# Attention's product with the values: from two half-array fp32 products to one full-array product of split operands

## Chip, core and metric

The kernel runs on one core of one Trainium2 chip, as one launch. The metric is the device time in microseconds (us) of that core, the median of several runs. Engines are named as in the profile: PE is TensorE (PEld its weight loads), DVE is VectorE, ACT is ScalarE, POOL is GpSimd, SP issues most of the DMAs.

## The reference, cut to what matters

The program is two small models in a row, both of width 1024 on 512 tokens, in float32: a block with windowed grouped-query attention, a block with retention (each followed by a gated feed-forward), and then two layers with a mixture of experts. Only the attention is touched. It has 16 query heads of 64 dimensions and 4 key/value heads; a block of 128 queries sees 256 context keys and up to three blocks of 128 local keys, and a sink column:

```python
s_ctx = einsum('bqkgd,bnkd->bkgqn', qb, k_c) * scale
s_loc = where(valid, einsum('bqkgd,bnkd->bkgqn', qb, kb) * scale, NEG_INF)
p = softmax(concatenate([s_ctx, s_loc, sink_col], axis=-1))
o = einsum('bkgqn,bnkd->bqkgd', p[..., :L], v_c) + einsum('bkgqn,bnkd->bqkgd', p[..., L:L + band], vb)
...
out_x = o_x @ w_o
```

The 256 context tokens are queries too (two more blocks, which see the context keys alone).

## The kernel before

**Split operands.** Most products are made from operands in two parts: `hi` is the value rounded to the type float32r, `lo` the remainder in the same type, and `mm3` adds up hi·hi, hi·lo and lo·hi in PSUM. `net.hilo(hi, lo, src)` makes the parts: ACT copies `src` into `hi`, then DVE subtracts `hi` from `src` into `lo`.

**Attention.** `Attention.heads` walks through 8 pairs of query heads (`pr`) and 6 query blocks (`b`) each, 48 blocks in all; `nk` is the number of local key blocks of a query block (2, 3, 3, 2, then 0 and 0 for the context). `nkt = 2 + nk` tiles of 128 keys follow, so a pair has 22 of them and the whole attention 176. The steps of a block:

- `scores`: PE writes the scores of both heads into the PSUM tile `sc`, of which there is one buffer (in pair 7 the last blocks use a smaller one). DVE takes the maximum (L1156) and three short operations on the tile `sm` (L1157 to L1159), ACT two exponentials (L1163) into `pt`; these are the last readers of `sc`.
- `weights`: two short DVE operations (L1171, L1172); then one head's weights are scaled on ACT (L1177), the other's on POOL (L1175).
- `values`: the weights are transposed on PE (L1192), up to two key tiles at a time into the PSUM tile `tr` (2 buffers), copied to `th` (ACT at L1197, or DVE at L1195 for the second piece), and multiplied with the values `vs` (L1205). There are 96 such pieces: 80 of 512 columns and 16 of 256. Then `hilo` splits the PSUM tile `po` into `oh` and `ol`.

The steps overlap: block n+1's scores are written before block n's `values`, and block n+1's `weights` are called from within it. `Fill` puts other PE work between them: the query projections of the next pair (L975 to L977, 3 x 8 matmuls), the projection of finished heads (`project`, L1127 on DVE), and adaptive-norm products (L491). The order in which each engine gets its instructions is set by the framework's scheduler when the program is built, so it can move when the costs of instructions change.

**The product at L1205** has one key tile's values of one group as weights, 128 keys by 64 columns in fp32. The two heads of a pair go to the array's two column halves (`tile_position=(0, 64 * s)`) and run beside each other. The program has 352 such matmuls; each fp32 one runs as two instructions of the trace, 704.

`begin` makes the values of the 6 token tiles in its generator `token_values`, and copies them out of PSUM at L1103.

Of the kernel before, what the change touches and what calls it, by code (L numbers as in the profile page):

```python
# [8 lines left out]
F32 = mybir.dt.float32  # L9
F32R = mybir.dt.float32r  # L10
BF = mybir.dt.bfloat16
I32 = mybir.dt.int32
AF = mybir.ActivationFunctionType
OP = mybir.AluOpType
# [4 lines left out]
S = 512  # L19
# [207 lines left out]
class Net:  # L227
    def __init__(self, ctx, tc, ins, out, taps=None):
        self.tc, self.nc, self.ins, self.out = tc, tc.nc, ins, out
        self.taps = taps or {}  # L230
        self.n = 0
        self.rings, self.st_rings = [], []
        self.ri, self.si = 0, {}
        self.clock, self.sides, self.inside = 0.0, [], False
# [698 lines left out]
class Attention:  # L933


    def __init__(self, net, hid, x, ctxT, gx, gc, fill, es, sp):
        self.net, self.hid, self.fill = net, hid, fill
        self.x, self.ctxT, self.gx, self.gc = x, ctxT, gx, gc
        self.wq = net.ins["attn_w_qkv"][0].rearrange("(k p) c -> p k c", p=128)
        self.wo = net.ins["attn_w_o"][0].rearrange("(k p) c -> p k c", p=128)  # L940
        self.op = es.enter_context(net.pool("attn_o"))
        self.es, self.ps_es, self.rope_es = ExitStack(), ExitStack(), ExitStack()
        self.ap = self.es.enter_context(net.pool("attn"))
        self.rp = self.rope_es.enter_context(net.pool("attn_rope"))
        self.sp = sp
        self.vs = [self.ap.tile([128, 4, 64], F32, name=f"vs{t}") for t in range(6)]
        self.small = False
        self.kh, self.kl, self.qs, self.qy, self.oh, self.ol = ({} for _ in range(6))

# [123 lines left out]
    def begin(self, first, ps_es):  # L1073

        net, nc = self.net, self.net.nc
        kw, qw = first
        wst = net.stage(self.wq[:, :, 1280:1536], 8, 256)
        pk, pq, pc = (self.sp.tile([128, S], F32, name=f"first{n}") for n in "kqc")
        ps = {1: (pk, pc[:, :L]), 0: (pq, pc[:, L:])}
        for g, (c0, n) in enumerate(GR):  # L1080
            for is_k, w in ((1, kw), (0, qw)):
                for us in self.product(ps[is_k][c0 // S][:, c0 % S:c0 % S + n], w, c0, n):
                    net.tick(us)
            if g == 0:
                self.consts()
                wv = net.split(wst[:, 0:4])
        rest = []
        for is_k, gain, then in ((1, "kg", self.keys_rest), (0, "qg", self.queries_rest)):
            if is_k:
                f, sq = (self.t(n, (128, NT), F32R, 3, self.op).bitcast(F32) for n in ("oh", "ol"))  # L1090
            else:
                f, sq = self.ftiles()
            self.take(ps[is_k][0], 0, S, f, sq, net.v(gain))
            self.take(ps[is_k][1], S, L, f, sq, net.v(gain))
            rest.append(then(0, f, sq))
        wv += net.split(wst[:, 4:8])
        rest = [net.side(r) for r in rest]

        def token_values():
            for t in range(6):  # L1100
                pv = net.ps()[:, :256]
                net.mm3(pv, [self.hid.at(k, t * 128, 128) + (wv[k // 4 * 2][:, k % 4], wv[k // 4 * 2 + 1][:, k % 4]) for k in range(8)])
                nc.scalar.activation(self.vs[t], pv.rearrange("p (g d) -> p g d", g=4), AF.Copy)  # L1103
                yield 2.6

        self.tv = self.fill.add(token_values(), -1)
        self.fill.pump(8.0)
        for r in rest:
            net.finish(r)
        ps_es.close()  # L1110
        self.sp = self.ps_es.enter_context(net.pool("attn_ps", space=PSUM))
# [67 lines left out]
    def values(self, pr, blkno, pt, beside, between=None):  # L1179
        net, nc, sp = self.net, self.net.nc, self.sp  # L1180
        q0, kb, nk, m0 = self.blocks[blkno]
        g, nkt = pr // 2, 2 + nk
        po = sp.tile([128, S], F32, name=net.nm("po"), tag="po")[:, :128]
        if blkno == 0:
            self.oh[pr] = self.t("oh", (128, NT), F32R, 3, self.op)
            self.ol[pr] = self.t("ol", (128, NT), F32R, 3, self.op)

        def turn(j0, n):
            tr = sp.tile([128, 2, 256], F32, name=net.nm("tr"), tag="tr", bufs=2)
            for j in range(j0, j0 + n):  # L1190
                for s, c in enumerate((j, j + 2 if j < nk else j - nk)):
                    nc.tensor.transpose(tr[:, j - j0, s * 128:s * 128 + 128], pt[s][:, c * 128:(c + 1) * 128], net.ident)  # L1192
            th = self.t("th", (128, 2, 256), bufs=3)
            if j0 == 2:
                nc.vector.tensor_copy(th[:, :n], tr[:, :n])  # L1195
            else:
                nc.scalar.activation(th[:, :n], tr[:, :n], AF.Copy)  # L1197
            return j0, n, th

        def take(j0, n, th):  # L1200

            for j in range(j0, j0 + n):
                v = self.vs[kb + j if j < nk else 4 + j - nk][:, g]
                for s in range(2):
                    nc.tensor.matmul(po[64 * s:64 * s + 64], v, th[:, j - j0, s * 128:s * 128 + 128],  # L1205
                                     start=(j == 0), stop=(j == nkt - 1), tile_position=(0, 64 * s))

        ready = []
        for j0 in range(0, nkt, 2):
            ready.append(turn(j0, min(2, nkt - j0)))  # L1210
            if j0 >= 2:
                take(*ready.pop(0))
        if between:
            between()
        self.fill.pump(beside)
        while ready:
            take(*ready.pop(0))
        net.hilo(self.oh[pr][:, q0:q0 + 128], self.ol[pr][:, q0:q0 + 128], po)

    def heads(self, beside, tail):  # L1220

# [50 lines left out]
def retention(net, hid, x_groups, before, freed, last, fill):  # L1272
# [3 lines left out]
    with ExitStack() as yes:  # L1276
# [201 lines left out]
        for hd in range(4):  # L1478
            tables(hd)
            qk(hd)  # L1480
            if hd:
                project(hd - 1)
                values(hd)
            pan = gate_panel(hd, 0)
            gated(hd, pan, attend())
# [563 lines left out]
def diff_attention(net, i, pool, sp, hh, hl, win, mix, V, lam_init, early, last):  # L2049
# [115 lines left out]
    for n, (hd, b) in enumerate(work):  # L2165
        if b == 0:
            fill.finish(nxt.get(hd))
            if hd == 0:
                fill.add(early, 1)
            if hd < 3:  # L2170
                nxt[hd + 1] = fill.add(project(hd + 1))
            if hd == 2:
                fill.finish(early)
        if (hd, b) == (3, 0):
            fill.add(last)
        ready.append((hd, b, scores(hd, b)))
        step_out()
        fill.pump(1.5 if hd < 3 else 1.8)
        if n:
            values(*ready.pop(0))  # L2180
    for r in ready:
        values(*r)
        step_out()
# [586 lines left out]
```

## Time and profile before

| | |
|---|---|
| median of 3 runs | 3113.56 us (3111.11 to 3114.87) |
| the profiled execution | 3106.33 us |
| its span, first to last instruction | 3104.2 us |
| mean granted clock of PE | 0.977 |
| PE busy over the span | 2939.8 us (95%) |
| blocks of the attention | about 88 to 445 us of the span |

The profile is of one execution, whose own time was 7 us below the median of the runs shown. A share of busy time is a mean over all stages, and the attention is about a ninth of the span.

### The profile page before, as it was taken

What the parts mean: (1) busy time and instruction counts of PE and PEld (TensorE: products, weight loads), DVE (VectorE), ACT (ScalarE), POOL (GpSimd) and SP (SyncE); (2) the same over time, 40 slices, a digit from 0 to 9 for tenths busy, and PEclk for the clock granted to TensorE, in tenths of its full rate; (3) what the DMA queues carried; (4) which work ended last, traced back from release to release, by engine and by line L of the source; (5) the groups of instructions that cost most, each with busy time, mean ns of one, the idle gap of its engine ahead of it and who ended that gap; (6) DMA issues with size and microseconds to landing.
All of it is one profiled execution on the core that took longest, in us unless ns stands there. A gap on an engine that the chain in (4) does not pass through costs nothing. (4 is left out here: it accounts for less than half of the span.)

```text
span 3104.2 us, 42345 instructions
## 1 busy us (share of the span) xinstructions
PE 2939.8 (95%) x16384; PEld 2427.0 (78%) x16384; DVE 1902.0 (61%) x3557; ACT 1298.5 (42%) x2227; POOL 406.0 (13%) x389
## 2 busy tenths in 40 slices
PE   6999989999999999999999999999999988999995
PEld 5777779888888888888887788877876767787663
DVE  5566575545552664535465543669778766988865
ACT  3655563121212432323243322436555543656544
POOL 1112130000000200000020000221212212121220
PEclk8999999999999999999999999999999989999997
DMA  6121133324441222223133432231469944146993
GB/s 223 49 74 55 49 98 100 116 89 129 144 142 55 88 67 82 78 67 98 37 114 117 125 127 96 89 119 41 133 201 362 351 161 121 35 153 226 378 352 142
DMA packets 307875, 410.18 MB, mean 132 GB/s; under 512 B 16655, under 2 KB 248207, under 8 KB 307025
## 3 DMA queue, kind: packets, MB, share of 16 engines
q1 hardware_dynamic: 293840, 357.03, 35.0%
q0 software_dynamic: 13824, 50.34, 4.5%
q8 instruction: 133, 2.18, 0.3%
q14 instruction: 78, 0.63, 0.1%
HBM read 379.01 MB, written 28.31 MB: 131 GB/s over the span
## 5 line engine op out<-in xcount | busy, mean ns | idle before, releaser
L308 ACT ACTIVATE hi<-st 128x1024 fp32r<-128x1024 f32 (+1 forms) x420 | 432.7, 1034 | 691.9 <-PE ps L369 497.6
L309 DVE TENSOR_TENSOR lo<-st,hi 128x1024 fp32r<-128x1024 f32 (+1 forms) x420 | 510.5, 1219 | 233.9 <-ACT hi L308 222.5
L368 PE MATMUL ps<-hxh,hi 128*128 128x512 f32 (+1 forms) x1280 | 477.3, 374 | 2.5 <-DVE sg L828 0.8
L369 PE MATMUL ps<-hxl,hi 128*128 128x512 f32 (+1 forms) x1280 | 475.3, 372 | 0.5 <-DVE hxl L645 0.5
L370 PE MATMUL ps<-hxh,lo 128*128 128x512 f32 (+1 forms) x1280 | 475.0, 371 | 0.0
L368 PEld LDWEIGHTS ps<-hxh,hi 128*128 128x128 f32 x1280 | 241.9, 189 | 52.2 <-ACT sg L827 5.6
L370 PEld LDWEIGHTS ps<-hxh,lo 128*128 128x128 f32 x1280 | 242.0, 189 | 42.4 <-issue 1.2
L369 PEld LDWEIGHTS ps<-hxl,hi 128*128 128x128 f32 x1280 | 242.1, 189 | 41.2 <-issue 1.2
L368 PE MATMUL ps<-ah,hi 128*128 128x256 f32 (+1 forms) x592 | 200.5, 339 | 3.2 <-DVE x L774 1.6
L369 PE MATMUL ps<-al,hi 128*128 128x256 f32 (+1 forms) x592 | 198.5, 335 | 0.2 <-DVE al L378 0.2
L370 PE MATMUL ps<-ah,lo 128*128 128x256 f32 (+1 forms) x592 | 198.4, 335 | 0.0
L774 DVE SCALAR_TENSOR_TENSOR x<-ps,vecs,x 128x512 f32<-128x512 f32 (+1 forms) x136 | 84.4, 623 | 147.9 <-PE ps L370 147.8
L828 DVE TENSOR_TENSOR sg<-sg,ps 128x512 f32<-128x512 f32 (+1 forms) x70 | 40.1, 572 | 187.0 <-PE ps L370 186.3
L593 POOL TENSOR_TENSOR nacc<-nacc,nsq 128x256 f32<-128x256 f32 x56 | 49.4, 883 | 594.7 <-ACT nsq L592 593.5
L368 PEld LDWEIGHTS ps<-ah,hi 128*128 128x128 f32 x592 | 111.4, 188 | 19.0 <-DVE x L774 3.6
L2571 PE MATMUL py<-st,at 128*128 128x512 f32 x272 | 123.0, 593 | 1.7 <-DVE y L2575 1.2
L369 PEld LDWEIGHTS ps<-al,hi 128*128 128x128 f32 x592 | 111.5, 188 | 12.6 <-DVE al L378 0.4
L370 PEld LDWEIGHTS ps<-ah,lo 128*128 128x128 f32 x592 | 111.3, 188 | 12.6
L2545 PE MATMUL pa<-hi,xt 128*128 128x512 f32 x288 | 118.5, 412 | 0.5 <-ACT xt L377 0.5
L368 PE MATMUL ps<-hch,hi 128*128 128x256 f32 x416 | 117.7, 283 | 0.6 <-DVE mod L527 0.5
L369 PE MATMUL ps<-hcl,hi 128*128 128x256 f32 x416 | 117.2, 282 | 0.0
L370 PE MATMUL ps<-hch,lo 128*128 128x256 f32 x416 | 117.1, 282 | 0.0
(671 smaller groups left out, 7065.7 us busy)
## 6 DMA issues: line engine op xcount, KB each, us to landing
st<-moe_w_dram SPq DMA_DIRECT2D x136, 512.0 KB
st<-ffn_w_in_dram SPq DMA_DIRECT2D x44, 1024.0 KB
st<-moe_w_dram SPq DMA_DIRECT2D x34, 1024.0 KB
ast<-ada_w_dram SPq DMA_DIRECT2D x56, 512.0 KB
st<-ret_w_qkvg_dram SPq DMA_DIRECT2D x24, 1024.0 KB
st<-ffn_w_out_dram SPq DMA_DIRECT2D x24, 768.0 KB
st<-ada_w_dram SPq DMA_DIRECT2D x12, 1024.0 KB
st<-w_in_dram SPq DMA_DIRECT2D x12, 1024.0 KB
```

The costliest lines, as they stand in the source:

```text
L308: self.nc.scalar.activation(h, v, AF.Copy)
L309: self.nc.vector.tensor_tensor(l, v, h.bitcast(F32), op=OP.subtract)
L368: self.nc.tensor.matmul(ps, wh, xh, start=(i == 0), stop=False)
L369: self.nc.tensor.matmul(ps, wh, xl, start=False, stop=False)
L370: self.nc.tensor.matmul(ps, wl, xh, start=False, stop=(i == n - 1))
L593: nc.gpsimd.tensor_tensor(self.acc, self.acc, sq, op=OP.add)
L774: net.nc.vector.scalar_tensor_tensor(xm, p, self.gate[:, m:m + 1], xm, op0=OP.mult, op1=OP.add)
L828: nc.vector.tensor_tensor(sg, sg, pu, op=OP.mult)
L2545: nc.tensor.matmul(pa, th[:, k], wh, start=(k == 0), stop=False)
L2571: nc.tensor.matmul(py[:, n * 512:n * 512 + 512], at[:, f], w2[f][:, 0, n * 512:n * 512 + 512], start=(f == 0), stop=(f == 1))
```

## The change

1. `vs` holds 128 columns for each token tile and group instead of 64: the values' `hi` part in columns 0 to 63 and the `lo` part in 64 to 127, made with `hilo`.
2. A transposed piece is split by `hilo` into `th` and `tl`: every piece now has one ACT copy and one DVE subtraction of its full width, where it had one copy on one of the two.
3. The product is two matmuls for each key tile, with the same weights (128 x 128), and moving 256 columns (both heads): one with `th`, one with `tl`. It writes a `po` of 128 x 256: the rows 0 to 63 hold the products with the values' hi part, 64 to 127 those with the lo part. All four terms are kept.
4. At the end of a block the two halves are added: for each head ACT copies one half of `po` into the new tile `ob` (one buffer), and DVE adds the other. `oh` is then copied from `ob` on ACT, and `ol` is subtracted on POOL.

```diff
-        self.vs = [self.ap.tile([128, 4, 64], F32, name=f"vs{t}") for t in range(6)]
+        self.vs = [self.ap.tile([128, 4, 128], F32R, name=f"vs{t}") for t in range(6)]
...
-                nc.scalar.activation(self.vs[t], pv.rearrange("p (g d) -> p g d", g=4), AF.Copy)
+                pv = pv.rearrange("p (g d) -> p g d", g=4)
+                net.hilo(self.vs[t][:, :, 0:64], self.vs[t][:, :, 64:128], pv)
...
-        po = sp.tile([128, S], F32, name=net.nm("po"), tag="po")[:, :128]
+        po = sp.tile([128, S], F32, name=net.nm("po"), tag="po")[:, :256]
...
-            th = self.t("th", (128, 2, 256), bufs=3)
-            if j0 == 2:
-                nc.vector.tensor_copy(th[:, :n], tr[:, :n])
-            else:
-                nc.scalar.activation(th[:, :n], tr[:, :n], AF.Copy)
-            return j0, n, th
-
-        def take(j0, n, th):
+            th, tl = (self.t(r, (128, 2, 256), F32R, bufs=2) for r in ("th", "tl"))
+            net.hilo(th[:, :n], tl[:, :n], tr[:, :n])
+            return j0, n, th, tl
+
+        def take(j0, n, th, tl):
...
-                for s in range(2):
-                    nc.tensor.matmul(po[64 * s:64 * s + 64], v, th[:, j - j0, s * 128:s * 128 + 128],
-                                     start=(j == 0), stop=(j == nkt - 1), tile_position=(0, 64 * s))
+                nc.tensor.matmul(po, v, th[:, j - j0], start=(j == 0), stop=False)
+                nc.tensor.matmul(po, v, tl[:, j - j0], start=False, stop=(j == nkt - 1))
...
-        net.hilo(self.oh[pr][:, q0:q0 + 128], self.ol[pr][:, q0:q0 + 128], po)
+        ob = self.t("ob", (128, 128))
+        for s in range(2):
+            a, b = self.HALVES[s]
+            cs = slice(s * 128, s * 128 + 128)
+            nc.scalar.activation(ob[a], po[b, cs], AF.Copy)
+            nc.vector.tensor_tensor(ob[a], ob[a], po[a, cs], op=OP.add)
+        oh, ol = (o[pr][:, q0:q0 + 128] for o in (self.oh, self.ol))
+        nc.scalar.activation(oh, ob, AF.Copy)
+        nc.gpsimd.tensor_tensor(ol, ob, oh.bitcast(F32), op=OP.subtract)
```

**What the change does to the order.** Behind the attention (PE's row 2214 of 14,562 before) the instructions of every engine stand in the same order as before; SP's queue differs only in where three of the loads of `ada_w` stand among the feed-forward's weights. Within the attention the scheduler moved rows. The lines of `values` have other numbers after the change: the transpose L1192 is L1193, the products are L1202 (with `th`) and L1203 (with `tl`), DVE's maximum L1156 is L1157, and so on by one; the copies and subtractions of a piece stand at the helper's lines L377 and L378, the two additions of a block at L1220.

PE in pair 0, block 1, from the last two transposes of the block's second piece on, before (`tr`, `th`, `po`, `vs` as above; `ps` is the next pair's query projection; x2 is a pair of half-array matmuls):

```order
L1192 MATMUL tr_884<-kident_69,pt_756 128x128
L1192 MATMUL tr_884<-kident_69,pt_757 128x128
L975 MATMUL ps_836<-hxh_110,hi_830 128x512
L1205 MATMUL po_876<-th_882,vs_344 64x128 x2
L1205 MATMUL po_876<-th_882,vs_345 64x128 x2
L1192 MATMUL tr_895<-kident_69,pt_756 128x128
L1192 MATMUL tr_895<-kident_69,pt_757 128x128
L976 MATMUL ps_836<-hxl_111,hi_830 128x512
L1205 MATMUL po_876<-th_889,vs_346 64x128 x2
L1205 MATMUL po_876<-th_889,vs_348 64x128 x2
```

and the same place of the change:

```order
L1193 MATMUL tr_901<-kident_69,pt_761 128x128
L1193 MATMUL tr_901<-kident_69,pt_762 128x128
L977 MATMUL ps_846<-hxh_110,lo_841 128x512
L1202 MATMUL po_891<-th_897,vs_344 128x256
L975 MATMUL ps_846<-hxh_110,hi_840 128x512
L976 MATMUL ps_846<-hxl_111,hi_840 128x512
L977 MATMUL ps_846<-hxh_110,lo_841 128x512
L975 MATMUL ps_846<-hxh_110,hi_840 128x512
L976 MATMUL ps_846<-hxl_111,hi_840 128x512
L1203 MATMUL po_891<-tl_898,vs_344 128x256
L1202 MATMUL po_891<-th_897,vs_345 128x256
L1203 MATMUL po_891<-tl_898,vs_345 128x256
```

The first product with `th` stands where it stood, the first with `tl` has five projection matmuls of 512 columns ahead of it.

DVE at the same place, from the maximum of block 2's scores to the reciprocal, before:

```order
L1156 TENSOR_REDUCE sm_851<-sc_852 128x2
L1195 COPY th_889<-tr_884 128x512
L1157 TENSOR_TENSOR sm_851<-sm_851,qys_590 128x2
L1158 TENSOR_TENSOR sm_851<-sm_851,nsink 128x2
L1159 TENSOR_TENSOR sm_851<-sm_851,nsink 128x2
L1171 TENSOR_TENSOR sm_851<-sm_851 128x2
L378 TENSOR_TENSOR ol_805<-po_876,oh_804 128x128
L1172 RECIPROCAL sm_851<-sm_851 128x2
```

and of the change:

```order
L1157 TENSOR_REDUCE sm_866<-sc_867 128x2
L378 TENSOR_TENSOR tl_898<-tr_892,th_897 128x512
L1158 TENSOR_TENSOR sm_866<-sm_866,qys_590 128x2
L378 TENSOR_TENSOR tl_907<-tr_901,th_906 128x512
L1159 TENSOR_TENSOR sm_866<-sm_866,nsink 128x2
L1160 TENSOR_TENSOR sm_866<-sm_866,nsink 128x2
L1172 TENSOR_TENSOR sm_866<-sm_866 128x2
L1173 RECIPROCAL sm_866<-sm_866 128x2
L378 TENSOR_TENSOR tl_918<-tr_914,th_917 128x256
```

Two subtractions of block 1's pieces now stand between the maximum of block 2's scores and the short operations that its exponentials wait for, where one copy stood; the subtraction that makes `ol` is gone from DVE here.

## Rows read from the trace of the kernel before

**Rows 1.** The page's head and its first part: busy time, share, instructions.

```profile
span 3104.2 us, 42345 instructions
PE 2939.8 (95%) x16384; PEld 2427.0 (78%) x16384; DVE 1902.0 (61%) x3557; ACT 1298.5 (42%) x2227; POOL 406.0 (13%) x389
```

**Rows 2.** Windows: the attention's blocks, then head pairs 0 and 4 (busy us).

```profile
88.00:445.00 357.00, 338.16 (x2494) 269.90 (x2493) 216.67 (x540) 208.73 (x497) 75.34 (x79) 0.98 0.20 63
...
90.50:131.10 40.60, 38.29 (x282) 30.12 (x282) 21.02 (x57) 24.31 (x60) 7.52 (x8) 0.96 0.22 66
...
270.40:316.50 46.10, 44.68 (x331) 37.77 (x329) 32.11 (x73) 25.03 (x58) 8.86 (x8) 1.00 0.17 52
```

The columns are the stretch, its length, the busy us of PE, PEld, DVE, ACT and POOL, the granted clock, the DMA share and GB/s.

**Rows 3.** Timeline of PE in pair 4: start, duration, line.

```profile
251.10 0.66 PE L1205 MATMUL po<-th,vs 128*64 128x128 f32 x8
251.69 0.38 PE L976 MATMUL ps<-hcl,hi 128*128 128x256 f32 x1
251.91 0.28 PE L977 MATMUL ps<-hch,lo 128*128 128x256 f32 x1
...
252.43 0.29 PE L1153 MATMUL sc<-kh,qs 128*128 128x256 f32 x1
252.64 0.44 PE L1205 MATMUL po<-th,vs 128*64 128x128 f32 x4
253.01 0.38 PE L1154 MATMUL sc<-kl,qs 128*128 128x256 f32 x1
253.23 0.28 PE L976 MATMUL ps<-hcl,hi 128*128 128x256 f32 x1
253.35 0.29 PE L977 MATMUL ps<-hch,lo 128*128 128x256 f32 x1
...
254.16 0.28 PE L975 MATMUL ps<-hch,hi 128*128 128x256 f32 x1
```

**Rows 4.** Instructions on tile po: count, min/median/max ns, first and last start.

```profile
L1205 PE MATMUL po<-th,vs x704: 272/273/476, 93.3 to 442.2; 128*64 128x128 f32 x176
```

**Rows 5.** Instructions on tile tr: prices of copies and subtractions from PSUM.

```profile
L378 DVE TENSOR_TENSOR xt<-tr,xt x72: 676/682/692, 2304.2 to 3045.1; 128x512 fp32r<-128x512 f32 x72
...
L2563 DVE COPY at<-tr x36: 412/420/427, 2316.5 to 3059.2; 128x256 f32<-128x256 f32 x36
L1195 DVE COPY th<-tr x32: 674/685/692, 93.5 to 430.5; 128x512 f32<-128x512 f32 x32
```

**Rows 6.** Groups by shape, 88 to 445 us: busy us, mean ns, idle before.

```profile
L378 DVE TENSOR_TENSOR ol<-po,oh 128x128 fp32r<-128x128 f32 x48 | 13.8, 288 | 14.4 <-ACT oh L377 14.2
...
L1197 ACT ACTIVATE th<-tr 128x512 f32<-128x512 f32 x48 | 28.5, 594 | 46.7 <-PE tr L1192 46.7
...
L377 ACT ACTIVATE oh<-po 128x128 fp32r<-128x128 f32 x48 | 12.9, 270 | 20.2 <-PE po L1205 19.8
...
L1000 POOL TENSOR_TENSOR qf<-qf,krc 128x512 f32<-128x512 f32 x8 | 13.8, 1719 | 28.8 <-DVE aux L999 16.2 <-DVE sm L1159 8.0 <-DVE sm L1157 4.6
...
L593 POOL TENSOR_TENSOR nacc<-nacc,nsq 128x256 f32<-128x256 f32 x14 | 10.4, 744 | 6.5 <-ACT nsq L592 5.7 <-DVE sm L1172 0.5
```

**Rows 7.** Waits of PE and PEld, 88 to 445 us: total us, times, longest.

```profile
PE sc L1149 <- ACT pt L1163: 7.4, 6, 1.9
...
PE po L1205 <- DVE th L1195: 2.8, 5, 0.7
PE po L1205 <- ACT th L1197: 1.9, 8, 0.3
...
PEld po L1205 <- ACT th L1197: 13.0, 29, 1.2
PEld sc L1149 <- ACT pt L1163: 10.1, 9, 2.0
...
PEld po L1205 <- DVE th L1195: 3.9, 5, 0.9
```

## The prediction

> **What bounds the kernel now.** I read the page first: PE is busy for 95% of a span of 3104.2 us, and DVE for 61% [rows 1]. Then the windows: in the attention's 357 us PE is busy for 338.2, DVE for 216.7, ACT for 208.7; a pair with little fill work (pair 0, 40.6 us) has DVE at 52% and ACT at 60%, one with a projection beside it (pair 4, 46.1 us) has DVE at 70% and PE still at 97% [rows 2]. So PE sets the pace, and a us of PE's work is a us of time as long as the other engines deliver. But "busy" counts a matmul's whole pipelined duration, so what a matmul costs is read from the timeline, as the distance of two starts. Last come the waits: PE and its loads wait for `th` for 21.6 us in 47 places (1.9 + 2.8 + 13.0 + 3.9), and for the exponentials that free `sc` for 17.5 us in 15 of the 48 blocks [rows 7]. The second number matters here: the score tile has one buffer, and the loop scores, maximum, exponentials, next scores is nearly as long as a block.
>
> **What the product costs on PE, before and after.** Full-array matmuls of 256 moving columns in a stream start 0.116 us apart (seven steps from 253.35 to 254.16) [rows 3]. A run of eight half-array instructions, two key tiles, takes 0.59 us to the next start (251.10 to 251.69), a run of four, one key tile, 0.37 us (252.64 to 253.01) [rows 3]. Each run also delays its neighbours: it starts 0.21 us after a 256-column matmul (252.43 to 252.64) where 0.116 is usual, and the matmul behind it is followed after 0.22 us (251.69 to 251.91, and 253.01 to 253.23) where 0.116 is usual [rows 3]. I read these as the array emptied, and a weight load exposed, when its division changes.
>
> After the change a key tile is two full-array matmuls of 256 columns like those of L976, so 0.232 us, and the runs have no borders. A long run loses 0.59 - 0.464 = 0.126, plus 0.094 and 0.104 at its borders: 0.324 us. A short one loses 0.37 - 0.232 = 0.138 and the same borders: 0.336. On the timeline of PE I counted 91 runs between 93.3 and 442.2 us, 65 of them of eight instructions and 14 of four [rows 4]. So **PE's work shrinks by 91 x 0.33 = 30 us**. The number of columns streamed does not shrink: within a run a key tile takes about 0.22 us (the difference of the two run lengths, 0.59 - 0.37), and 0.232 after. All of the gain is borders.
>
> One rule speaks against this. The Trainium skill, "TensorEngine Tiling (Array Packing)", sections "The Problem" to "When to Use Tiling", says that weights of 64 columns or fewer leave half the array unused and that column tiling gains up to 2x. By it, giving the halves up would double 176 x 0.22 = 39 us of products: some 39 us slower, 3153; I give that 0.02 of the slower cases' chance. The rows don't bear that out for this change, since the free half is filled with the values' low part and both heads share one stream; I take the 0.232. The weights change only at every second matmul, fewer than in L975 to L977, which hold 0.116, so no extra load is priced (its worst, the 0.22 of an exposed one at each of 352, would be +36 us).
>
> **What is added on the other engines.** DVE: 80 subtractions of 512 columns at 0.682 and 16 of 256 at about 0.42, less 32 copies at 0.685 [rows 5]: 54.6 + 6.7 - 21.9 = +39.4; 96 additions of 128 columns at the 0.288 of `ol`, less 48 of those [rows 6]: +13.8; six for `vs` at 0.42: +2.5. In all +55.7, to 272 us of 357, 76%. ACT: 32 more copies at 0.594 and 96 copies of 128 columns at 0.270 (`oh` remains) [rows 6]: +19.0 + 25.9 = +45, to 254 us, 71%. If the 64-partition operations cost half, DVE has 14 and ACT 13 us less; I take the full price, as the column count is the same as in those rows. POOL: 48 subtractions of 128 columns, between a quarter of 1.719 and half of 0.744 [rows 6], about 0.4 us, 19 us in all on an engine that is busy for 75 of 357 [rows 2]. Behind `ol` on POOL stands the scaling of a later block's weights; `ol` itself is read by a projection blocks later, so it hides.
>
> If every engine were free to run ahead, none of these would cost time: PE's rest, about 357 - 30 us, is longer than 272 or 254. Pair 4 shows that DVE at 70% lets PE run at 97% [rows 2]. What costs is order, in two places.
>
> *Waits for the pieces.* A product with `tl` waits for one more step, 0.682 us and a handover of some 0.05. Counting in the order, at the prices above, the PE work that stands between a piece's last transpose and its first use: median 1.4 us before, and 2.1 us to the first use of `tl`. So +0.73 needed, +0.66 covered by fill work; 0.07 x 96 = 7 us is the upper end, nothing the lower (uses of `th` now have more cover than before). I take +3.
>
> *The score loop.* In DVE's order, between the maximum and the third short operation, there stood 9 copies of `th` and 12 subtractions of `ol` over the 48 blocks, 9.6 us; after the change 24 subtractions of `tl` and 38 additions of `ob`, 24 x 0.682 + 38 x 0.288 = 27.3 us. So the loop grows by 17.7 us, 0.37 per block, while PE's part of a block shrinks by 30 / 48 = 0.62. In the 15 blocks in which PE already waited for the loop [rows 7], PE's gain is lost and the growth is paid: 15 x 0.62 + 15 x 0.37 = 15 us. The ends: nothing, if the loop's slack takes it; all 48 blocks, 48 x 0.99 = 47 us. I take +15.
>
> The six extra DVE operations for `vs` lie in the start, before the first scores; 1 us at most, left out. Behind the attention nothing moves.
>
> **Sum.** -30 + 3 + 15 = **-12 us**. The profiled execution (3106.3) would come to 3094; it was 7 us below the median of the runs, so the median goes from 3113.6 to **3101.5**.
>
> **Rivals.**
> - *PE's whole gain arrives* (-22 to -30 us, 3084 to 3092): the scheduler's fill covers `tl`, and the loop has slack. For it: pair 4 [rows 2]. Against: PE waited for `sc` in 15 blocks while DVE and ACT were at about 60%. Chance 0.17.
> - *Given back to the last few us* (within 0.2%, which is 6 us and about what a measurement here can tell from no change; 3107 to 3120): the score loop binds in 21 to 33 blocks instead of 15, at 0.62 + 0.37 each 21 to 33 us for the +15. For it: in the light pairs PE and ACT come close, in pair 0 ACT's 24.3 + 5.6 us against PE's 40.6 - 3.75. Chance 0.18.
> - *Slower*: evacuation becomes the bound. From block to block runs a second loop: transposes, `th`, `tl`, product, `ob`, and behind `ob` in ACT's queue the scaling of the next block's weights, which its transposes need. It grows by 0.73 for `tl`, and by about 0.5 since ACT now copies both pieces and copies `po` twice (0.270): 1.25 us per block. Where it binds, a block pays 1.25 instead of gaining 0.62; from 16 of the 48 blocks on the gain is gone, and with 24 the sum is +15, 3128. Against it: on ACT and DVE it holds 0.594 + 0.594 + 0.682 + 0.54 us and the scaling [rows 5, 6], while a block lasts 357 / 48 = 7.4 us. Chance 0.2. The Trainium skill states such an end: "TensorEngine Tiling (Array Packing)", "PSUM Bottleneck", says that the copy out of PSUM may become the bottleneck when the product gets faster, and that both ScalarE and VectorE should be used for it, as is done here; the trace before shows neither above 70%.
>
> **How the numbers follow.** The forecast, 3093 to 3107, has 0.45. Faster by over 0.2%: 0.45 + 0.17 = 0.62; same 0.18; slower 0.20. The range of 8 in 10 goes from 3087 (half of the first rival below it) to 3118 (half of the slower case above it), which leaves out about 0.18. The likeliest case's own range is 3093 to 3107.
>
> **What would show it right or wrong.** Right: L1202 and L1203 follow their neighbours after 0.12 us with no 0.2 us borders; the window of the attention is some 12 us shorter and the rest unchanged; waits for `tl` and `th` sum to about 25 us; waits for `sc` grow from 17.5 us to about 25 to 30. Wrong: products at 0.2 us or more apart; `sc` waits at 17 us or below (then the whole gain arrives); waits of the transposes on ACT or POOL that were not there (then the slower case); DVE's subtraction with one PSUM operand above 0.7 us.

## The result and the profile after

The change makes the kernel slower: 3129.14 us, the median of 6 runs (3127.21 to 3137.16), against 3110.96 us for 6 runs of the kernel before. The ratio is 1.0059, with a 95% interval of 1.0048 to 1.0070, so some 18 us. The prediction was 12 us faster.

The profiled execution took 3129.62 us, its span is 3127.4. First its page:

```profile
PE 2942.8 (94%) x16032; PEld 2442.9 (78%) x16032; DVE 1954.8 (63%) x3675; ACT 1342.4 (43%) x2355; POOL 428.2 (14%) x437
```

PE has 352 instructions less and is busy 3 us longer [rows 1]. The window of the attention, which now ends at about 462 us, has the columns of [rows 2]:

```profile
88.00:462.00 374.00, 342.13 (x2149) 288.69 (x2147) 266.88 (x657) 252.25 (x625) 97.11 (x127) 0.95 0.18 59
```

The window is 17 us longer; from the first transpose to the last product the attention is 14 us longer (table below). DVE has 50 us more and ACT 44, near what the prediction counted (55.7 and 45), and neither is near full: 71% and 67%. The granted clock fell from 0.98 to 0.95. Next the groups by shape that answer to [rows 5, 6]:

```profile
L378 DVE TENSOR_TENSOR tl<-tr,th 128x512 fp32r<-128x512 f32 x80 | 53.8, 686 | 8.3 <-ACT th L377 6.5
L1220 DVE TENSOR_TENSOR ob<-ob,po 64x128 f32<-64x128 f32 x96 | 27.2, 284 | 19.2 <-ACT ob L1219 17.0
...
L377 ACT ACTIVATE th<-tr 128x512 fp32r<-128x512 f32 x80 | 45.5, 594 | 25.7 <-PE tr L1193 25.6
...
L1219 ACT ACTIVATE ob<-po 64x128 f32<-64x128 f32 x96 | 26.0, 271 | 36.7 <-PE po L1203 23.5 <-DVE ob L1220 11.0 <-PE sc L1154 0.9
...
L1223 POOL TENSOR_TENSOR ol<-ob,oh 128x128 fp32r<-128x128 f32 x48 | 24.4, 508 | 89.6 <-ACT oh L1222 62.7 <-ACT sm L1165 21.9 <-PE ps L370 5.0
```

The prices on DVE and ACT came out as taken from the rows of before (0.682, 0.288, 0.594 and 0.270 us); POOL's `ol` takes 0.51 where the prediction put about 0.4. What an instruction costs was not the error; the error lies in when it can start. The waits, as in [rows 7] (total, times, longest); a wait that holds a matmul and its weight load appears in both rows, in part for the same time:

```profile
PE po L1203 <- DVE tl L378: 9.9, 14, 2.5
PE sc L1150 <- ACT pt L1164: 6.6, 8, 2.2
...
PEld po L1203 <- DVE tl L378: 16.4, 21, 2.7
PEld sc L1150 <- ACT pt L1164: 9.5, 11, 3.1
PEld po L1202 <- ACT th L377: 8.2, 22, 0.8
...
PEld tr L1193 <- ACT pt L1178: 2.9, 6, 0.7
PEld tr L1193 <- ACT ob L1219: 2.3, 2, 1.5
```

Counted once where the two rows hold the same time, the waits for `th` and `tl` are 24.6 us in 43 places, where those for `th` were 17.0 us in 34. Those of the first score matmul of a block (L1150, L1149 before) for the exponentials that free `sc` are 9.5 us in 11 blocks where they were 10.1 in 9: the score loop did not get worse. The longest single waits have grown from 1.2 us to 2.7 at the products. One of them on PE's timeline:

```profile
154.16 0.39 PE L1203 MATMUL po<-tl,vs 128*128 128x256 f32 x1 [2.13 <-DVE tl L378]
154.39 0.28 PE L1202 MATMUL po<-th,vs 128*128 128x256 f32 x1
154.51 0.28 PE L1203 MATMUL po<-tl,vs 128*128 128x256 f32 x1
```

The products themselves do what was forecast: 154.39 to 154.51 is 0.12 us, without borders. But PE stands still for 2.13 us, and the matmul behind the wait is followed only after 0.23 us (154.16 to 154.39). DVE around that time:

```profile
151.91 0.42 DVE L1061 TENSOR_SCALAR qys<-nry 128x12 f32<-128x12 f32 x1 [1.10 <-POOL nry L384]
...
152.44 0.95 DVE L1069 TENSOR_TENSOR qs<-qf,qs 64x768 fp32r<-64x768 f32 x1
153.42 1.29 DVE L378 TENSOR_TENSOR tl<-tr,th 128x512 fp32r<-128x512 f32 x2
```

`th` of the first piece was ready at 151.60, but the two `tl` stand in DVE's order behind the norms of the next pair's queries (`qys`, `qs`). DVE is idle for 1.10 us there, until POOL has the inverse roots (`nry`). Before the change the same wait of 1.10 us stood in the same place (150.80 on DVE), with one copy `th` and one short `sm` operation behind it instead of two subtractions, and PE waited for that copy for 0.41 us. The idle time is only a part of the 2.13 us: `qs` (0.95 us), which stood behind the copy before, now stands ahead of both `tl`. And behind the standstill, in windows again:

```profile
154.20:156.00 1.80, 1.80 (x16) 1.80 (x16) 0.51 (x1) 1.00 (x3) 0.00 (x0) 0.98 1.05 408
155.90:159.30 3.40, 3.40 (x12) 1.93 (x11) 2.28 (x12) 1.85 (x5) 0.69 (x1) 0.51 0.65 240
```

PE is busy without a gap from 154.20 on, yet from 155.90 to 159.30 it was granted 0.51 of its clock, the lower of its two levels (1.2 GHz). So the wait is paid again in part. The Trainium skill, "TensorE: Matmul & The Clock Gate", section "HAM oscillation — how this bites in real kernels", describes a loop in which each wait for a DMA is followed by matmuls at the throttled clock. The rows here agree that half clock follows a wait; the wait is one for DVE, though, and the fall comes 1.7 us after its end.

**PE's time in the attention** can be split along its timeline. The distance of two starts, less the price of the first in a stream (0.116 us for 256 columns, 0.229 for 512, and so on), goes to the wait or border between them, to the half clock where that was granted, or to a load that shows behind a wait. From the first transpose to the last product, in us of the profiled execution (one each, so a few us are chance; work includes the waits of the L491 products for their weights):

| kernel | work | borders | waits | behind a wait | half clock | rest | stage |
|---|---|---|---|---|---|---|---|
| before | 286.9 | 23.0 | 26.9 | 2.4 | 5.5 | 5.5 | 350 |
| after | 287.9 | 3.1 | 41.8 | 7.2 | 17.4 | 6.9 | 364 |
| pe_alone | 284.9 | 3.3 | 28.4 | 6.4 | 8.7 | 6.8 | 338 |
| load | 290.4 | 20.4 | 33.7 | 4.3 | 10.6 | 6.3 | 365 |
| less_pe | 265.3 | 20.5 | 29.3 | 2.7 | 4.9 | 5.1 | 328 |
| qys_pool | 284.2 | 3.1 | 38.9 | 7.4 | 8.7 | 6.7 | 349 |
| one_run | 288.2 | 16.3 | 26.4 | 3.6 | 8.8 | 6.8 | 350 |
| one_qys | 284.6 | 16.7 | 21.3 | 3.6 | 3.9 | 7.4 | 338 |

The kernels below before and after are the experiments. Stages are compared, not spans, because the first projection starts at 42 to 43 us or at 48 in the profiles, whatever the kernel, and because the part behind the last product takes 2661.8 us (before) to 2678.5 us (no_ob) in the 20 profiles, though the change moves nothing there. The profile of before has the shortest such part of all.

### The profile page after: what moved, and what is told of

Read it like the earlier page. It is cut to its first block, busy times and chain, and to the rows that moved or that the text cites. A ratio compares the mean times of both kernels' runs of the same rounds, so it can differ in the third digit from the quotient of the medians.

```text
span 3127.4 us, 41953 instructions
## 1 busy us (share of the span) xinstructions
PE 2942.8 (94%) x16032; PEld 2442.9 (78%) x16032; DVE 1954.8 (63%) x3675; ACT 1342.4 (43%) x2355; POOL 428.2 (14%) x437
## 3 DMA queue, kind: packets, MB, share of 16 engines
q8 instruction: 130, 2.13, 0.3%
## 5 line engine op out<-in xcount | busy, mean ns | idle before, releaser
L2550 PE MATMUL pa<-hi,xt 128*128 128x512 f32 x288 | 119.0, 413 | 0.5 <-ACT xt L377 0.5
L2551 PE MATMUL pa<-hi,xt 128*128 128x512 f32 x288 | 117.0, 406 | 0.0
## 6 DMA issues: line engine op xcount, KB each, us to landing
st<-moe_w_dram SPq DMA_DIRECT2D x34, 1024.0 KB, 10.2
```

The costliest lines, as they stand in the source:

```text
L2550: nc.tensor.matmul(pa, th[:, k], wh, start=(k == 0), stop=False)
L2551: nc.tensor.matmul(pa, tl[:, k], wh, start=False, stop=False)
```

## The experiments

All were timed beside runs of the kernel before on the same chip. "Half clock" is what PE lost to it in a run on the average, (1 - mean granted clock) x span. It counts the whole program; the part behind the attention alone has 55 to 69 us of it in the 20 profiles.

| run | median us | ratio to before, 95% interval | half clock us |
|---|---|---|---|
| before, 34 runs | 3111.83 | 1 | 73.7 |
| after | 3129.14 | 1.0059 [1.0048, 1.0070] | 83.9 |
| pe_alone | 3103.25 | 0.9973 [0.9962, 0.9984] | 75.9 |
| no_tl | 3105.83 | 0.9987 [0.9975, 0.9999] | 75.8 |
| no_ob | 3111.10 | 1.0000 [0.9989, 1.0012] | 74.1 |
| one_run | 3107.97 | 0.9989 [0.9979, 0.9999] | 71.2 |
| load | 3130.10 | 1.0058 [1.0039, 1.0078] | 82.9 |
| late | 3131.28 | 1.0054 [1.0036, 1.0071] | 88.3 |
| th_dve | 3123.23 | 1.0039 [1.0027, 1.0052] | 77.3 |
| late_dve | 3140.01 | 1.0077 [1.0060, 1.0095] | 93.6 |
| lo_pool | 3146.26 | 1.0098 [1.0082, 1.0115] | 92.2 |
| lo_th | 3132.48 | 1.0061 [1.0048, 1.0074] | 83.3 |
| before_pool | 3127.47 | 1.0043 [1.0027, 1.0058] | 81.8 |
| pause | 3131.18 | 1.0054 [1.0040, 1.0068] | 82.6 |
| less_pe | 3090.27 | 0.9930 [0.9917, 0.9943] | 75.4 |
| dve_light | 3137.56 | 1.0081 [1.0068, 1.0094] | 89.0 |
| scale_light | 3128.87 | 1.0050 [1.0033, 1.0066] | 83.9 |
| qys_pool | 3119.98 | 1.0024 [1.0010, 1.0038] | 80.5 |
| qys_th | 3119.90 | 1.0022 [1.0012, 1.0032] | 80.4 |
| one_qys | 3103.22 | 0.9971 [0.9960, 0.9982] | 76.7 |

**The parts of the change.** `pe_alone` has the new product with the evacuation of before:

```diff
-            net.hilo(th[:, :n], tl[:, :n], tr[:, :n])
-            return j0, n, th, tl
+            if j0 == 2:
+                nc.vector.tensor_copy(th[:, :n], tr[:, :n])
+            else:
+                nc.scalar.activation(th[:, :n], tr[:, :n], AF.Copy)
+            return j0, n, th, th
...
+        net.hilo(self.oh[pr][:, q0:q0 + 128], self.ol[pr][:, q0:q0 + 128], po[:, :128])
```

> Left out: the pieces are copied once (float32r, on ACT or DVE as in the kernel before), the second product of a key tile takes the same piece again instead of its low part, and the end of a block splits half of po as before; so PE does the changed kernel's matmuls and the other engines the work of before. Theory A (PE's 30 us are real, and the evacuation's added steps take them back): 22 to 30 us faster than before, about 3083, waits for th near the 21.6 us of before. Theory B (the full-array product gains nothing in place, its starts come 0.2 us apart after each wait, or the blocks are paced by another loop): within 8 us of before. If A holds the remaining 40 to 48 us up to the changed kernel are the evacuation's.

8 us faster, far from theory A's 22 to 30. `no_tl` keeps the new end of a block and copies the pieces once (the first hunk above alone):

> Left out: the low part of the transposed pieces (copied once as before, and the product takes the piece twice); the end of a block is that of the change, with ob. Theory A1 (the price is the second step of each piece, tl): at most 8 us above the run with PE's change alone, so 14 us or more faster than before. Theory A2 (the price is the end of a block, ob on ACT and DVE twice, oh, ol): within 8 us of the changed kernel, about 3125. Theory B: near the changed kernel too, whatever is left out.

4 us faster than before. `no_ob` splits the pieces and ends a block as before (the last line above alone):

> Left out: the addition of the two halves of po; the end of a block splits the first 128 columns as before, the pieces are split into th and tl as in the change. Theory A1 (tl is the price): within 8 us of the changed kernel. Theory A2 (ob is the price): 14 us or more faster than before. If the two prices add, this run and the one without tl lie together 40 to 48 us above twice the run with PE's change alone.

The same as before, so neither theory A1 nor A2 holds. The product brings 8 us, the end of a block costs 4, the subtractions 8, but both together 26. The prices do not add up; whether it is the engines' load, a chain or the order that makes the two dear together, these runs do not tell.

The evacuation alone, `load`: the product of before, which waits for `th` only, with the copies, subtractions and additions of the change beside it.

```diff
-            if j0 == 2:
-                nc.vector.tensor_copy(th[:, :n], tr[:, :n])
-            else:
-                nc.scalar.activation(th[:, :n], tr[:, :n], AF.Copy)
+            tl = self.t("tl", (128, 2, 256), bufs=2)
+            nc.scalar.activation(th[:, :n], tr[:, :n], AF.Copy)
+            nc.vector.tensor_tensor(tl[:, :n], tr[:, :n], th[:, :n], op=OP.subtract)
...
+        ob, od = self.t("ob", (128, 128)), self.t("od", (128, 128))
+        for s in range(2):
+            a, b = self.HALVES[s]
+            nc.scalar.activation(ob[a], po[a], AF.Copy)
+            nc.vector.tensor_tensor(od[a], ob[a], po[a], op=OP.add)
```

> The product of before (half-array, waits for th alone) with the evacuation work of the change put beside it: both pieces copied on ACT, a subtraction tl that nobody reads on DVE, the four-step end of a block (its addition a duplicate, its result unread). Theory Q (the change costs time because a product must wait for a longer chain of queued steps): with the product not waiting for tl, only the second pieces' copies, now behind the exponentials on ACT, come late; +2 to +8 us over before, 3113 to 3120. Theory L (the load on ACT and DVE itself costs the time, through the score loop and the fill's own evacuation): what the two additions cost on top of the product alone, +26 us, comes without the dependence too: 3132 to 3140.

18 us slower than before: as much as the change loses, with no product that waits for `tl`. Theory Q as put there falls, and the time is just under theory L's range. Its waits:

```profile
PE po L1204 <- DVE od L1221: 4.1, 3, 2.3
PE tr L1192 <- ACT pt L1177: 3.6, 6, 1.3
```

The added steps hold PE at other places, too: the next product waits until `od` has read `po`, transposes wait for the scaling of their weights.

**Is it load on the engines, a block's chain, or the order?** One thing limits what these runs can tell: the scheduler orders each kernel anew. Compared by line and tile up to the end of the attention, 7% of PE's rows stand elsewhere than in the changed kernel in `dve_light`, 8% in `scale_light`, 11% in `th_dve` and 20% in `late`, so each is also another order. `late` puts fill work ahead of a block's first products:

```diff
-            if j0 >= 2:
-                take(*ready.pop(0))
+            if j0 == 2 and nkt > 4:
+                beside /= 2
+                self.fill.pump(beside)
+                take(*ready.pop(0))
```

> The changed kernel with the fill work of a block put ahead of its first products (in blocks of five key tiles half of it ahead of the first, half ahead of the others). Theory Q: in the changed kernel 19.8 us of the waits for th and tl fall on pieces that are not the last of their block and have only the next transposes as cover; most of that goes, and with it some stretches at half clock: 8 to 16 us faster than the changed kernel, 3113 to 3121. Theory L: the load is the same, so the time is the same, 3125 to 3133.

No gain: PE waits for `tl` 6.9 us instead of 9.9, but 2.0 instead of 0.7 for `lo` of the fill's weights and 3.8 instead of 1.4 or so for the scaled weights of the transposes, and it loses more to half clock. `th_dve` puts the copy of each second piece on DVE again (the condition `j0 == 2` as above, the subtraction on DVE behind it):

> The changed kernel with the copy th of each second piece on DVE again, as before the change. Theory Q: the copies' time behind exponentials on ACT (51 us in the changed kernel, 29 before) falls back; but second pieces are mostly the last of their block and covered (2 us of waits), and DVE gets 22 us more work ahead of tl: 0 to 5 us faster than the changed kernel, 3124 to 3129. Theory L (DVE, the busier engine, is what costs): 4 to 10 us slower, 3133 to 3139.

6 us faster than the change, although DVE has 22 us more; the copies stand less behind the next block's exponentials on ACT (about 51 us in all after the change, 24 here), which need not be the cause. `late_dve` has both edits:

> Both edits of the two kernels before this one. Theory Q: the first piece is covered by the fill, so only the last pieces' chain counts, and it is shorter with the exponentials not in its way: 10 to 20 us faster than the changed kernel, 3109 to 3119. Theory L: 3125 to 3139.

The slowest of these, so the two edits do not add up either. `dve_light` takes DVE work away that is no step of a block:

```diff
-                nc.vector.scalar_tensor_tensor(x[:, m], p, gate[:, m:m + 1], x[:, m], op0=OP.mult, op1=OP.add)
+                nc.vector.scalar_tensor_tensor(x[:, m, :64], p[:, :64], gate[:, m:m + 1], x[:, m, :64], op0=OP.mult, op1=OP.add)
```

> The changed kernel with the projections' additions into x and ctxT (L1128) cut to 64 of their 512 or 256 columns: some 20 us less on DVE, none of it a step of a block; the rest of the residual is left out. Theory Q (work of any kind in DVE's in-order queue costs): 6 to 14 us faster than the changed kernel, 3115 to 3124. Theory S (only a block's own chain counts): 3126 to 3132.

Not faster but 8 us slower. DVE has 18 us less (248.9 in its attention), and the standstill shown above is there to the hundredth of a us:

```profile
156.21 0.42 DVE L1061 TENSOR_SCALAR qys<-nry 128x12 f32<-128x12 f32 x1 [1.10 <-POOL nry L384]
...
157.72 1.29 DVE L378 TENSOR_TENSOR tl<-tr,th 128x512 fp32r<-128x512 f32 x2
```

On PE the product behind it waits 2.13 us again. Less work on DVE does not shorten a standstill that the order makes. `scale_light` shortens each block's chain instead:

```diff
-            else:
-                nc.scalar.activation(pt[s][:, :w], pt[s][:, :w], AF.Copy, scale=sm[:, 6 + s:7 + s])
```

> The changed kernel with the first head's weights not scaled by 1 / sum (ACT, 48 instructions, 33 us, each a step of its block between the sums and the transposes); that scaling is left out. Theory S: a step of 0.5 to 0.83 us less in each block's chain, 12 to 25 us faster than the changed kernel, 3105 to 3118. Theory Q in the form that DVE's queue is what costs: at most 6 us faster, 3123 to 3130, since DVE's work stays.

No gain in time, with 33 us less on ACT: transposes now wait for POOL's scaling of the other head (4.2 us), which stands in the same place of the chain. So the edit does not shorten the chain by what was expected, and the chain is not ruled out. What these runs show is that the time does not follow DVE's or ACT's busy time: 18 us less on DVE came out slower, 22 us more faster.

**Work moved to POOL.** `lo_pool` puts the subtraction of the weights' split on POOL during the attention:

```diff
-        self.nc.vector.tensor_tensor(l, v, h.bitcast(F32), op=OP.subtract)
+        e = self.nc.gpsimd if getattr(self, "lo_pool", False) else self.nc.vector
+        e.tensor_tensor(l, v, h.bitcast(F32), op=OP.subtract)
```

> The changed kernel with the subtraction lo of the weights' split on POOL while the attention runs (16 instructions of 128x1024, 1.275 us each, 20 us off DVE's queue; no step of a block itself is touched). Theory D (pieces and scores wait behind other work in DVE's in-order queue, and long standstills bring half clock): 5 to 12 us faster than the changed kernel, 3117 to 3125, with fewer standstills of PE over 0.8 us than its 11. Theory E (a block's own added steps on ACT and DVE make it longer, whatever stands between them): no gain, 3127 to 3133; slower still if the scaling of pt on POOL now stands behind lo.

`lo_th` has this edit on `th_dve`, `before_pool` on the kernel before:

> lo_pool with the copy of each second piece on DVE, as in th_dve (3123). Theory D: both gains, 3111 to 3118. Theory E: that of th_dve alone, 3121 to 3126.

> The kernel before with lo on POOL as in lo_pool: what that edit is worth without the change. Theory D: DVE has 61% of the attention there, few waits end on it: 0 to 4 us faster than before, 3107 to 3112. Theory E: the same as before, 3110 to 3114, or slower by the scalings that come late on POOL.

All three miss. On POOL the instruction takes 2.39 us instead of 1.28, PE waits for `lo`, and the kernel before alone gets 14 us slower by it. The weights of the fill now come late, so the edit says nothing on DVE.

**Does PE's work count one to one, and what does a standstill cost?**

```diff
-            nc.tensor.matmul(p, wl[:, k], xh, start=False, stop=(k == 7))
+            if not thin:
+                nc.tensor.matmul(p, wl[:, k], xh, start=False, stop=(k == 7))
```

> The kernel before with PE work of the size that the change takes out, taken from the fill: the third term (weights' low part) of the query and key projections inside the attention is left out, 128 matmuls of 512 and 256 columns, 64 x (0.229 + 0.116) = 22 us, some 0.46 us per block; no wait, copy or border is touched. Theory P (PE sets the pace, and what the product alone fails to bring is lost by its own edit): 18 to 22 us faster than before, 3090 to 3094. Theory S (a block's chain through ACT and DVE is nearly as long as its PE work, so that PE's work is worth less than 1:1 wherever it is taken): 6 to 12 us faster, 3100 to 3106, with more waits in the attention than before's 27 us.

20.7 us of 22: theory P. PE sets the pace, and a us of its work taken out of the fill is nearly a us of time, although the scheduler moved 17% of the rows that remain on PE. `pause` puts standstills in:

```diff
+                if blkno == 3 and pr:
+                    for _ in range(6):
+                        nc.gpsimd.tensor_scalar(pt[s][:, :w], pt[s][:, :w], 1.0, 1.0, op0=OP.mult, op1=OP.mult)
```

> The kernel before with standstills put in: in the fourth block of seven pairs POOL multiplies its weights by 1 six times more (6 x 0.69 = 4.2 us), of which PE's other work covers an unknown part, so seven standstills of some 0.5 to 3 us. Theory C (a long standstill of PE is paid again by the stretch at half clock behind it): stretches at half clock of 3.4 us or more behind most standstills over 1.2 us, and the time over before is the sum of the standstills plus half of those stretches. Rival: the stretches come by chance, as many as before (about 147 us in all), and the time grows by the standstills alone.

18 us slower, of which 8 are half clock (82.6 for the 75.0 of the runs of before beside it). But of the four long standstills that POOL's added work made in the profile (1.35, 1.95, 2.00 and 2.20 us) the first two had no such stretch behind them, in the third the clock fell while PE still stood, and only the fourth had one close behind. So theory C is not shown for each standstill. Over the attention of all 20 profiles, of 60 idle times of PE over 1.6 us 49 have a fall of the clock within them or in the 3 us behind, of 190 between 0.4 and 0.8 us 26; and 92 of the 108 falls have one of 0.8 us or more so close ahead. Long ones are often dearer than their length, by a factor that these runs leave open.

`one_run` is the kernel before with all pieces of a block transposed before the first product, so 64 runs of half-array products instead of 91:

```diff
-            if j0 >= 2:
-                take(*ready.pop(0))
         if between:
```

> Nothing left out. The kernel before, with all pieces of a block transposed before the first product, so that a block's half-array products stand closer: in the order 64 runs instead of 91. Theory A (borders of the half-array runs cost 0.2 us each and more, and PE sets the pace): 27 x 0.2 = 5 us faster or more, up to 9, if no new waits come. Theory B (another loop sets the pace): no change or slower, since the first product starts later.

3.4 us faster, with an interval of 0.3 to 6.5 us, so less than the 5 us of theory A: borders and their loads fall from 23.0 to 16.3 us in the split of PE's time, and the waits stay.

**Taking one wait out of DVE's order.** `qys_pool` is the changed kernel with the two short scalings on POOL, behind the inverse root that they need:

```diff
-        nc.vector.tensor_scalar(ys[:, 0], y, 0.125, None, op0=OP.mult)
-        nc.vector.tensor_scalar(ys[:, 1], y, -0.125, None, op0=OP.mult)
+        nc.gpsimd.tensor_scalar(ys[:, 0], y, 0.125, 1.0, op0=OP.mult, op1=OP.mult)
+        nc.gpsimd.tensor_scalar(ys[:, 1], y, -0.125, 1.0, op0=OP.mult, op1=OP.mult)
```

> The changed kernel with the two scalings of the query norms (qys, 128x12, 8 pairs) on POOL, right behind the rsqrt there that DVE now waits for with tl in its queue. Theory H (the loss sits in places where tl or the row maximum stands behind a step that waits): the standstills of 2.1 and 2.5 us at the products go, and stretches at half clock with them, 6 to 12 us faster than the changed kernel, 3117 to 3123. Rival K (tl is late wherever it stands, another step takes the place): 3126 to 3132.

`qys_pool` falls into theory H's range: 3119.98, a ratio of 1.0024 where the change had 1.0059, some 10 us. 14 instructions of 3.3 us in all moved in the attention, only 1% of PE's rows stand elsewhere, and DVE's busy time in the attention did not fall (269.7 us). At the place shown above:

```profile
147.90 0.95 DVE L1069 TENSOR_TENSOR qs<-qf,qs 64x768 fp32r<-64x768 f32 x1
148.88 1.29 DVE L378 TENSOR_TENSOR tl<-tr,th 128x512 fp32r<-128x512 f32 x2
```

`tl` stands right behind `qs`, without DVE's idle 1.10 us, and on PE the standstill is 0.54 us:

```profile
149.63 0.39 PE L1203 MATMUL po<-tl,vs 128*128 128x256 f32 x1 [0.54 <-DVE tl L378]
...
286.97 0.39 PE L1203 MATMUL po<-tl,vs 128*128 128x256 f32 x1 [0.94 <-DVE tl L378]
```

The second row is the place where the changed kernel has its longest standstill at a product, 2.51 us. In neither place does the clock fall now. The profiled execution was the fastest of the six, so the 15 us by which its stage is shorter are more than the edit is worth.

The same edit on `th_dve`:

> The same with the copy of each second piece on DVE, as in th_dve (3123). Theory H: 4 to 9 us below th_dve, 3114 to 3119. Rival K: 3121 to 3126.

No better than `qys_pool` (3119.90), just above theory H's range. And on `one_run`:

> The kernel before with one run of products per block, as in one_run (3108), and qys on POOL. Theory H: before the change nothing of a block's copies stands long behind qys, 0 to 3 us below one_run, 3105 to 3108. Rival K: as one_run, 3106 to 3110.

0.9971, some 9 us faster than before, and below theory H's 3105 to 3108. Nothing is left out in it, and it beats both kernels. Against `one_run` (0.9989) the edit brings some 5 us, with 0.2% of PE's rows in another place, and `qys_th` gains as much against `th_dve`. So about half of the 10 us in `qys_pool` is worth something without the change, too; the intervals of these differences are about 5 us to either side, and the edit was not run on the kernel before alone. That kernel has the same idle time of DVE in seven places:

```profile
L1061 DVE TENSOR_SCALAR qys<-nry 128x12 f32<-128x12 f32 x7 | 1.2, 173 | 12.2 <-POOL nry L384 12.2
```

## Why the prediction was wrong

In the profiles' stage (350 to 364 us) the sum came out as: work and borders -19 us, waits +15, loads behind waits +5, half clock +12, rest +1. The steps of the prediction one by one:

- **"PE's work shrinks by 91 x 0.33 = 30 us": the step that was mis-sized first.** The new product runs as forecast, at 0.12 us. But products and borders together fell by 22 us, not 30 (42.9 + 23.0 to 40.7 + 3.3, pe_alone in the split of PE's time). 3.3 us of borders remain. The 0.33 was read where PE streams, and some of the 91 runs begin behind a wait for `th` (34 places), where a border may cost less; this was not tested. And of the 22 only 8 arrive in the medians, 12 in the profile's stage, while 22 taken elsewhere (less_pe) arrive nearly whole. Of what is lost, the profile shows 4.0 us as loads that now show behind waits, 3 at half clock and 1.5 as waits; the rest is within the spread of single profiles and stays open.
- **"Waits for the pieces ... I take +3": mis-sized, and its picture failed.** The step counted one subtraction (0.73) against cover (0.66) as if `th` and `tl` started at once. From the end of a piece's last transpose to the end of its last copy the median was 0.75 us before and is 2.11 after (mean 1.31 and 2.56), +1.3: the copies stand behind the next block's exponentials on ACT (about 51 us in all instead of 29), and a `tl` starts 0.59 us after its `th` on the average, of which DVE is idle for a fifth, mostly held by an earlier instruction. The waits for the pieces grew by 8 us counted once (17.0 to 24.6), in PE's split time all waits by 15.
- **"The score loop ... I take +15": it did not happen.** Waits for `sc` are 16.1 us over both rows, 17.5 before. The prediction named 17 or below as the sign that the whole gain arrives; that inference was wrong too. The reading under the term was wrong as well: it added the waits of PE and of its weight loads, which are in part the same. Six of the 15 waits are the other nine seen again, so 9 blocks waited, for 10.1 us; the term would have been +9 and the forecast 18 us faster. The 21.6 us in 47 places for `th` are 17.0 in 34 in the same way.
- **What no term held: half clock.** It comes to 10 us of the 18 (83.9 for 73.7, averages over the runs), and to 12 in the stage of the profiles. The prediction priced every wait at its own length.
- **The rival that gave 3128** had the right sign and sum, and the right place: evacuation, which costs 18 us beside the old product (load) and 26 beside the new. Its mechanism, a loop from block to block on ACT and DVE that binds in 24 blocks, was not shown and not ruled out. The sign that the prediction named for it, new waits of the transposes on ACT, did appear, but small: 2.9 us for the scaled weights (0.3 before) and 2.3 for `ob`, on PE's weight loads, while 2.5 us for `qs` went away. Against it, 10 us came back by an edit outside that loop (qys_pool). What is shown is narrower: where an instruction that PE waits for stands in DVE's order behind one that itself waits, PE stands still, and taking one such wait out brings some 10 us. Since the same edit brought some 5 us on `one_run`, which has no such loss, perhaps 5 of the 26 us are accounted for, at most 10; the others (row maxima of 1.49 us ahead of `tl`, exponentials ahead of `th`) were seen in the trace and not tried singly, so the cause of most of the loss stays open.
- The Trainium skill warns in "TensorEngine Tiling (Array Packing)", section "PSUM Bottleneck", that the copy out of PSUM may become the bottleneck; its case is a product made four times faster by tiling. Here the copies did undo the gain of a product that got only a little faster, with DVE at 71% and ACT at 67%.
- The reason given against that rival, a block's 7.4 us against 2.3 us of evacuation, was an average. It says nothing on when a single copy can start.

## What to carry to other kernels

When a step is added between two engines, don't price it at its duration: read on the consumer's side how long an instruction stands in the queue from the moment that its input is there, and find the instructions in that queue that wait for a third engine. One such wait ahead of a critical copy could be moved for nothing here, and that was worth about as much as the new product. A gain of PE counted nearly one to one when it was taken from the fill, and for little more than a third when the product itself was exchanged, so measure it in place. And count a wait once where the profile shows it for the matmul and for its weight load. A few long standstills of PE are to be feared more than many short ones, since the clock often falls behind them.

## What the hardware did that was not expected

- PE's granted clock fell to half for 3.4 to 10.2 us soon after most long standstills (49 of 60 over 1.6 us), even when PE was busy without a gap again (0.51 from 155.90 to 159.30 us): 10 us of the change's 18 on the average.
- A weight load of about 0.1 us shows behind a wait (0.23 instead of 0.12 to the next start, 154.16 to 154.39). In the split of PE's time this is 2.4 us before and 7.2 after, some 24 and 72 cases at 0.1 us; the 0.22 us behind a half-array run, which the prediction counted as its border, may be the same.
- An operation on 64 partitions costs what one on 128 does: 0.284 us for 128 columns (DVE, `ob`) and 0.271 (ACT), for 0.288 and 0.270 with 128 [rows 6].
- POOL needs 2.39 us for the subtraction of 128x1024 from SBUF for which DVE needs 1.28.
